# First-phase transfers in program order, planner durations read from the trace, and zeros in shorter gaps

## The chip, the core and the metric

The kernel runs on one core of a Trainium2 chip. The metric is the device time of one execution in microseconds; the time before is the median of three runs, and one further execution was profiled. All matrix work is in 32-bit floats, most of it on TensorE in the rounded form fp32r, where each product is made from three matmuls of split operands.

## The reference, cut to what matters

Two layers of a trunk over 256 latent and 256 context tokens with 1024 features. `c` and `c_ctx` modulate each half of the tokens through nine vectors per layer.

```python
mod_lat = split((silu(c) @ w_mod[l] + b_mod[l]), 9)          # likewise mod_ctx from c_ctx
def macaron_half(x, mods, gain, w_in, w_out):
    shift, scale, gate = mods
    h = modulate(rms_norm(x, gain), shift, scale)
    gate_, up = split(h @ w_in, 2)                            # FFN_DIM = 2816
    return x + 0.5 * gate * ((silu(gate_) * up) @ w_out)
for l in range(2):
    x   = macaron_half(x,   mod_lat[0:3], ...)                # first FFN, both streams
    ctx = macaron_half(ctx, mod_ctx[0:3], ...)
    y_lat, y_ctx = hybrid_mixer(...)                          # 8 attention heads + 4 gated delta-rule heads
    x = x + mod_lat[5] * (y_lat @ w_out[l])
    x = macaron_half(x, mod_lat[6:9], ...)                    # second FFN (context too in layer 0)
```

So before the first FFN matmul the kernel needs the norm statistics of `x`, and the first two modulation vectors (shift and scale), which take 8 MB of `w_mod`.

## The kernel before, in words

**A recorder and a planner.** The program text doesn't issue instructions. `Recorder` notes each instruction as a node with its engine, its duration by `cost_of` and its dependencies; `Schedule.run` then plays all engines forward in modelled time (durations from `cost_of`, the time from one engine's end to another's start from `LAT`, TensorE's two speeds from `Clock`) and picks, whenever an engine is free, the ready node with the lowest priority number. For TensorE this is its rank; for the other engines it is a due time worked back from the matmuls that need the result (`due_times`). `plan` does this 7 times with 3 window sizes and keeps the plan that ends first in the model. `emit` then issues all nodes sorted by their planned start. On the chip each engine runs its own list in that order and waits on semaphores, so the planned times themselves are gone: only the order on each engine, and the buffer that each tile got, remain. All DMAs are issued from the one list of SyncE (SP); a modelled DMA keeps "sync" busy for its bytes at the modelled rate, and its readers may start `LAT["sync"]` later.

**Zeros.** Where the plan leaves TensorE idle for longer than `WARM[1]` us, `keep_warm` puts matmuls of a zero tile (256 columns, counted at 0.109 us each) over a share `WARM[2]` of the gap, to hold the clock up.

**The first phase** is laid out by `main` and the start of `program`. `x` comes in 8 transfers of 256 KB; `square_sum`, `norm_stats` and `norm_spread` make the norm factors `bs`. `features(q, d, n)` handles n blocks of 128 features: `mods_first` loads its share of the first two modulation vectors' weights (4 or 8 transfers of 256 KB into `n` tiles), multiplies them with `sc` (the silu of `c`, from the small `cc` transfer), copies the result out on ScalarE, transposes it, adds the bias from `sm` (the transfer `small`) and scales the gain into `na` on VectorE; `norm_apply` then makes the FFN's operand `h` of these features, split into `hh` and `hl` (tag `s`). There are five such calls: two of one block, three of two. In between, `load(part, units)` brings quarters (256 KB) of the first FFN's input weights for units 0, 1 and 2, which ScalarE (`wh`) and VectorE (`wl`) split. The first group of `ffn` then multiplies feature block by feature block: 48 products of three matmuls each, 6 for each of the 8 blocks, of which blocks 2p and 2p+1 need the quarter `part` = p.

**The order of the first phase's DMAs before** is the planner's: by due time, not by the order in the text.

**The other stretches.** After the first phase come the first FFN, the mixer (attention and delta rule, with many small steps on ScalarE and VectorE between the matmuls), the second FFN, and the same for layer 1. While the FFNs run, `mods` fills in the other modulation vectors: 512 KB of `w_mod` for each of 128 pieces into a `wr` buffer (4 buffers, shared with all weights), reduced on VectorE into `md` by `tensor_tensor_reduce` (the rows show it as CUSTOM_DVE_ANT_0 with output `junk`). At the end of an FFN `add_x`, `square_sum` and `norm` make the next operand.

**Constants.** `con` holds ten constant matrices; the last, `mbd`, is read by nothing.

Lines of the rows: all recorded instructions are issued from one line (680), zeros from line 672. Tiles are named by their tag, so `ps<-n,sc` is the modulation matmul of the first phase, `ps<-s,wh` and `ps<-s,wl` the FFN's.

Of the kernel before, what the change touches and what calls it, by code (L numbers as in the profile page):

```python
# [87 lines left out]
def consts():  # L88
    i = np.arange(128)
    m, j = i[:, None], i[None, :]  # L90
    b, c = m // 32, j // 32
    mats = [
        m == j, m >= 0 * j,
        m > j, m < j, m <= j, m >= j,
        b == c, (b != c) & (b // 2 == c // 2), b // 2 != c // 2,
        b % 2 == c % 2,
    ]
    return np.concatenate([a.astype(np.float32) for a in mats], axis=1)

# [129 lines left out]
class Recorder:  # L229
# [3 lines left out]

    def __init__(self, cost):
        self.nodes, self.classes, self.open, self.cost = [], {}, None, cost
        self.tag, self.ahead = None, 0
        for e in self.ENGINES:
            setattr(self, e, Engine(self, e))

# [38 lines left out]
    def add(self, eng, ops):  # L278
        n = Node()
        n.i, n.eng, n.ops, n.preds, n.succs, n.syms = len(self.nodes), eng, ops, set(), [], []  # L280
        n.table, n.tag, n.ahead = None, self.tag, self.ahead
        n.cost = sum(self.cost(eng, *o) for o in ops)
        n.port = shares_port(eng, *ops[0])
        n.columns = sum(columns_of(*o) for o in ops) if eng == "tensor" else 0
        writes, reads = [], []
        for name, args, kw in ops:
            views = [a for a in list(args) + list(kw.values()) if isinstance(a, View)]
            outs = [a for a in (args[0], kw.get("accum_out")) if isinstance(a, View)]
            writes += outs
            reads += [v for v in views if all(v is not o for o in outs)]  # L290
            if name == "matmul" and not kw["start"]:
                reads.append(args[0])
            if name == "activation":
                n.table = TABLES.get(args[2].name)
        for v in reads:
            self.read(n, v)
        for v in writes:
            self.write(n, v)
        if eng == "tensor":
            for v in writes:  # L300
                if v.sym.group is not None:
                    n.preds.add(v.sym.group)
                v.sym.group = n.i
        n.preds.discard(n.i)
        for p in n.preds:
            self.nodes[p].succs.append(n.i)
        for v in reads + writes:
            if v.sym not in n.syms:
                n.syms.append(v.sym)
                v.sym.nodes.append(n.i)  # L310
        self.nodes.append(n)
# [58 lines left out]
class Pool:  # L370
# [16 lines left out]
    "vector": {"tensor": 0.2, "vector": 0.13, "scalar": 0.13, "gpsimd": 0.16, "sync": 0.13},  # L387
    "scalar": {"tensor": 0.27, "vector": 0.14, "scalar": 0.14, "gpsimd": 0.17, "sync": 0.14},
    "gpsimd": {"tensor": 0.25, "vector": 0.1, "scalar": 0.1, "gpsimd": 0.1, "sync": 0.1},
    "sync": {"tensor": 2.1, "vector": 2.1, "scalar": 2.1, "gpsimd": 2.1, "sync": 2.1},  # L390
}


WARM = (0.8, 0.6, 0.7)
SLACK = 0.2


# [21 lines left out]
class Schedule:  # L419


    def __init__(self, rec, rank, window, due=None):
        self.rec, self.rank, self.window = rec, rank, window
        self.prio = [r - n.ahead for r, n in zip(rank, rec.nodes)]
        if due:
            self.prio = [d if n.eng != "tensor" else p for p, d, n in zip(self.prio, due, rec.nodes)]
        self.start = [None] * len(rec.nodes)
        self.end = [None] * len(rec.nodes)

# [214 lines left out]
def keep_warm(rec, sched, cls):  # L644
# [6 lines left out]
    pe = sorted((sched.start[n.i], sched.end[n.i]) for n in rec.nodes if n.eng == "tensor")  # L651
    out, last = [], WARM[0]
    for a, b in pe:
# [68 lines left out]
def cost_of(eng, name, a, kw):  # L722

    views = [v for v in list(a) + list(kw.values()) if isinstance(v, View)]
    size = lambda v: int(np.prod(v.shape[1:]))
    if name == "dma_start":
        byts = 512 * max(size(v) * v.shape[0] // 128 for v in views if v.shape)
        return max(0.48, byts / 359e3) if eng == "sync" else 1.04
    if eng == "tensor":
        if name == "transpose":  # L730
            return 0.1095
        n = size(a[2])
        if "float32r" in str(a[2].sym.dtype):
            return 0.12 + max(n - 256, 0) * 0.000437
        if kw.get("tile_position", (0, 0))[1]:
            return 0.02
        return max(2 * n, 256) / 1200 + 0.01
    n = max([size(v) for v in views])
    points = sum(1 for v in views[1:] if size(v) == 1) if n > 1 else 0
    psum = any(v.sym.cls[1] == "ps" for v in views)  # L740
    if eng == "vector":
        if name == "reciprocal":
            return 0.068 + n / 160
        rate = 1920 if name in ("tensor_scalar", "tensor_copy") and not psum else 960
        if name == "memset":
            return 0.01 + n / 960
        return 0.068 + n / rate + 0.06 * min(points, 1)
    if eng == "scalar":
        return (0.05 if psum else 0.093) + n / 1200 + 0.093 * points
    if name == "memset":  # L750
        return 0.03 + n / 1185
    return 0.148 + n / 475
# [41 lines left out]
class Build:  # L794
# [35 lines left out]
    def open(self, ctx):  # L830
        tc, nc = self.tc, self.nc
        F32 = self.F32
        M = self.bass.MemoryType
        rec = self.nc

        def pool(name, bufs, **kw):
            p = ctx.enter_context(tc.tile_pool(name=name, bufs=1, **kw))
            make = lambda shape, nm, dt: p.tile(shape, dt, name=nm, tag=nm, bufs=1)
            return Pool(rec, make, bufs, kw.get("space") == M.DRAM)

        cp = self.cp = pool("cp", 1)
        self.lp = pool("lp", 2)
        self.wp = pool("wp", 1)
        self.sp = pool("sp", 1)
        self.tiny = pool("tiny", 4)
        self.ps = pool("ps", 8, space=M.PSUM)
        self.dram = pool("dram", 2, space=M.DRAM)
        con = self.con = cp.tile([128, 9 * 128 + 64], F32, name="con")
        c = [con[:, 128 * i:128 * i + 128] for i in range(9)]
        self.ident, self.ones, self.gt, self.lt, self.le, self.ge, self.mblk, self.m32, self.m64 = c  # L850
        self.mbd = con[:, 1152:1216]
        self.rope = cp.tile([128, 2, TL], F32, name="rope")
        self.junk = cp.tile([128, D], self.BF16, name="junk")
        self.eps = cp.tile([128, 1], F32, name="eps")
        zero = cp.tile([128, 256], self.BF16, name="zero")
        nc.vector.memset(zero, 0.0)
        nc.idle_work(zero, (id(self.ps), "ps"), F32)
        self.x = [None] * KD

    def load_const(self):  # L860
        nc = self.nc
        nc.sync.dma_start(self.con[:, 256:], self.io["consts"][:, 256:1216])
        nc.sync.dma_start(self.rope, self.io["rope"].rearrange("p (a b) -> p a b", b=TL))
        self.gtlt = self.cp.tile([128, 2, 128], self.F32R, name="gtlt")
        nc.scalar.copy(self.gtlt, self.con[:, 256:512].rearrange("p (a b) -> p a b", a=2))
# [998 lines left out]
    def main(self):  # L1864
        nc = self.nc
        self.acc = {}
        self.cond()
        lc = self.layer_consts(0)
        for d in range(KD):
            self.x[d] = self.slot("x", "x")  # L1870
            nc.sync.dma_start(self.x[d], self.io["xt"][:, d])
        nc.sync.dma_start(self.con[:, :256], self.io["consts"][:, :256])
        for d in range(KD):
            for s in (1, 0):
                self.square_sum(d, s, (nc.vector, nc.gpsimd)[s])
        self.wv.spawn(self.program(lc), 5)
        self.wv.run()

    def program(self, lc):
# [17 lines left out]
        def load(part, *units):  # L1897
            for f in units:
                self.weight_part(u[f][-1], self.io["w1_in"][0, f, part // 2], part % 2)

        def features(q, d, n):
            self.mods_first(lc, q, d, n)
            with self.nc.urgent(100):
                for i in range(2 * q + d, 2 * q + d + n):
                    for s in range(2):
                        self.norm_apply(lc, 0, s, i, bs[s])
        load(0, 0)
        features(0, 0, 1)
        load(0, 1, 2)
        features(0, 1, 1)  # L1910
        load(1, 0, 1, 2)
        features(1, 0, 2)
        for f in range(2):
            u[f].append(self.weight_begin())
        load(2, 0, 1)
        features(2, 0, 2)
        load(3, 0, 1)
        features(3, 0, 2)
        self.load_const()
        yield 0.0, 0.0  # L1920
        for l in range(L):
# [3 lines left out]
            a, b, c = f"a{l}" if l else "a", f"b{l}", f"c{l}"  # L1925
# [37 lines left out]
```

## Time and profile before

| | |
|---|---|
| median of 3 runs | 1949.0 us (1946.32 to 1955.2) |
| the profiled execution, its own time | 1952.2 us |
| its span, first to last instruction | 1950.4 us |
| mean granted TensorE clock | 0.991 |
| TensorE matmul busy | 1901.5 us (97%), 11145 matmuls |
| VectorE busy | 1366.0 us (70%) |
| ScalarE busy | 833.3 us (43%) |
| moved by DMA | 281 MB, 144 GB/s over the span |

Busy time of TensorE includes the zeros. Share of busy time is to be read by stage: in the first 40 us DMA is near its full rate, in the FFNs TensorE never stops, in the mixers VectorE and ScalarE are nearly full at times.

### The profile page before, as it was taken

The numbers are of one execution on the slowest core, as the hardware profiler recorded it, in microseconds if no ns is written. First come the engines' busy times: TensorE is split into PE (matmuls) and PEld (weight loads), VectorE is DVE, ScalarE is ACT, GpSimd is POOL, SyncE is SP. The second block draws the span as 40 slices with busy tenths as digits, with TensorE's granted clock in tenths as the row PEclk, the third lists the DMA queues.
The fourth block names the chain that finished last, engine by engine and source line by source line (L and its number), as shares of the span: only waits on it lengthen the run. The fifth ranks groups of instructions, "written<-read, shape, count | busy, mean of one in ns | idle before, by whom it ended". The sixth has DMA issues, their size and how long they took to land.

```text
span 1950.4 us, 29083 instructions
## 1 busy us (share of the span) xinstructions
PE 1901.5 (97%) x11145; PEld 1617.4 (83%) x11145; DVE 1366.0 (70%) x2776; ACT 833.3 (43%) x1612; POOL 26.9 (1%) x31
## 2 busy tenths in 40 slices
PE   8999999999999999999999999999999989899999
PEld 5888887787886879888888898888889877689999
DVE  5666677799987978666653586556337988986555
ACT  5322221258838455222222342221125974755433
POOL 1000000000001000000000000000000000000000
PEclk9999999999998999999999999999999999999999
DMA  9555555553324213555553245656334243136654
GB/s 329 179 153 160 162 177 175 170 169 117 112 81 117 98 44 95 165 162 179 166 162 102 72 146 179 201 177 203 110 98 147 88 114 109 44 114 201 184 182 122
DMA packets 104474, 280.96 MB, mean 144 GB/s; under 512 B 27024, under 2 KB 30480, under 8 KB 104336
## 3 DMA queue, kind: packets, MB, share of 16 engines
q1 hardware_dynamic: 104336, 279.12, 45.9%
q8 instruction: 87, 1.43, 0.3%
q14 instruction: 51, 0.42, 0.1%
HBM read 270.69 MB, written 8.39 MB: 143 GB/s over the span
## 4 chain that ended last, share of the span: by engine, by line
PE 76%; DVE 13%; ACT 4%; DMA 4%; issue 2%; SPq 0%; DVEq 0%; ACTq 0%
PE ps L680 76%; DVE d L680 3%; DVE n L680 2%; DMA wr<-w_mod 2%; DVE wl L680 2%; ACT d L680 1%; DVE wh L680 1%; ACT n L680 1%; DVE junk L680 1%; ACT wh L680 1%; DVE t L680 1%; DVE s L680 1%; DVE x L680 1%; ACT s L680 1%; ACT L680 1%
## 5 line engine op out<-in xcount | busy, mean ns | idle before, releaser
L680 PE MATMUL ps<-s,wh 128*128 128x512 f32 (+1 forms) x3344 | 912.9, 361 | 1.0 <-DVE s L680 0.5
L680 PEld LDWEIGHTS ps<-s,wh 128*128 128x128 f32 x3344 | 592.8, 189 | 100.3 <-issue 1.4
L680 PE MATMUL ps<-s,wl 128*128 128x512 f32 (+1 forms) x1672 | 603.5, 361 | 0.9 <-DVE wl L680 0.9
L680 ACT CAST wh<-wr 128x1024 fp32r<-128x1024 f32 (+2 forms) x341 | 350.4, 1037 | 479.1 <-PE ps L680 328.6
L680 DVE TENSOR_TENSOR wl<-wr,wh 128x1024 fp32r<-128x1024 f32 (+2 forms) x341 | 408.3, 1208 | 97.1 <-ACT wh L680 93.6
L680 DVE CUSTOM_DVE_ANT_0 junk<-wr,m,sm 128x1024 bf16<-128x1024 f32 x224 | 287.6, 1284 | 235.0 <-DMA wr<-w_mod 231.9
L680 PEld LDWEIGHTS ps<-s,wl 128*128 128x128 f32 x1672 | 314.8, 188 | 48.6 <-DVE wl L680 1.6
L680 PE MATMUL ps<-d,wh 128*128 128x256 f32 (+1 forms) x1344 | 300.4, 319 | 6.9 <-DVE x L680 3.9
L680 PEld LDWEIGHTS ps<-d,wh 128*128 128x128 f32 x1344 | 223.1, 191 | 30.3 <-issue 9.3
L680 PE MATMUL ps<-d,wl 128*128 128x256 f32 (+1 forms) x672 | 212.8, 317 | 1.2 <-DVE wl L680 1.2
L680 PE MATMUL ps<-n,wh 128*128 128x512 f32 (+1 forms) x640 | 178.3, 365 | 0.0
L680 DVE SCALAR_TENSOR_TENSOR x<-ps,hg,x 128x256 f32<-128x256 f32 x224 | 97.4, 478 | 93.2 <-PE ps L680 93.1
L680 ACT ACTIVATE d<-ps 128x512 f32<-128x512 f32 (+2 forms) x108 | 56.9, 529 | 237.1 <-PE ps L680 236.7
L680 PE MATMUL ps<-wh,s 128*128 128x512 f32 (+1 forms) x544 | 154.2, 360 | 0.3 <-DVE s L680 0.3
L680 PEld LDWEIGHTS ps<-d,wl 128*128 128x128 f32 x672 | 128.3, 191 | 9.5 <-DVE wl L680 1.7
L680 PEld LDWEIGHTS ps<-n,wh 128*128 128x128 f32 x640 | 115.4, 189 | 20.8
L680 PE MATMUL ps<-n,wl 128*128 128x512 f32 (+2 forms) x416 | 130.6, 347 | 0.7 <-DVE n L680 0.7
L680 DVE TENSOR_TENSOR d<-d,d 128x256 f32<-128x256 f32 (+29 forms) x310 | 111.6, 381 | 16.6 <-ACT d L680 12.0
L680 PEld LDWEIGHTS ps<-wh,s 128*128 128x128 f32 x544 | 96.4, 188 | 19.5 <-issue 5.2
L680 PE MATMUL ps<-wl,s 128*128 128x512 f32 (+1 forms) x272 | 96.6, 355 | 0.6 <-DVE wl L680 0.6
L680 DVE TENSOR_TENSOR d<-d,ps 128x512 f32<-128x512 f32 (+1 forms) x88 | 54.4, 618 | 58.4 <-PE ps L680 40.6
L680 PEld LDWEIGHTS ps<-n,wl 128*128 128x128 f32 x416 | 71.9, 189 | 10.7 <-issue 0.8
(163 smaller groups left out, 1563.7 us busy)
## 6 DMA issues: line engine op xcount, KB each, us to landing
wr<-w_in SPq DMA_DIRECT2D x171, 512.0 KB, 4.3
wr<-w_mod SPq DMA_DIRECT2D x128, 512.0 KB, 4.0
wr<-w_out SPq DMA_DIRECT2D x104, 512.0 KB, 4.2
wr<-wd SPq DMA_DIRECT2D x24, 512.0 KB, 3.8
n<-w_mod SPq DMA_DIRECT2D x32, 256.0 KB, 5.5
wr<-wg SPq DMA_DIRECT2D x8, 528.0 KB, 3.6
xd<-x SPq DMA_DIRECT2D x16, 256.0 KB, 4.5
x<-xd SPq DMA_DIRECT2D x16, 256.0 KB, 3.6
```

Of the source, the lines that this page charges most:

```text
L680: getattr(eng, name)(*[rv(x) for x in a], **{q: rv(x) for q, x in k.items()})
```

## The change

- `nc.settled` marks the SyncE nodes from the start of `main` to the last `load`: their priority is their place in the text (minus 1e6), ahead of all other DMAs. So these transfers are issued in program order.
- That order is written anew: the first block's modulation weights come first, then the quarters of all three units, then the second block's, and so on; `cc` and `small` come ahead of `x`.
- `LAT["sync"]` goes from 2.1 to 2.8 us (2.1 for DMA after DMA), the modelled DMA rate from 359 to 330 GB/s.
- `cost_of` is changed for the reduction `tensor_tensor_reduce` (from 0.13 to 0.19 us ahead of the elements), for VectorE copies and scalings on fewer than 128 partitions or at most 32 elements (half rate), and for ScalarE on 32 partitions (0.1 us more).
- Gaps longer than 0.3 us (before: 0.6) are filled with zeros, over 85% (before: 70%) of their length.
- `mbd` is dropped: `con` and its transfer are 64 columns narrower (32 KB of 480 KB).

```diff
@@ Recorder
+        self.tag, self.ahead, self.settled = None, 0, False
+        n.settled = self.settled and eng == "sync"
@@ LAT, WARM
-    "sync": {"tensor": 2.1, "vector": 2.1, "scalar": 2.1, "gpsimd": 2.1, "sync": 2.1},
+    "sync": {"tensor": 2.8, "vector": 2.8, "scalar": 2.8, "gpsimd": 2.8, "sync": 2.1},
-WARM = (0.8, 0.6, 0.7)
+WARM = (0.8, 0.3, 0.85)
@@ Schedule
+        self.prio = [n.i - 1e6 if n.settled else p for p, n in zip(self.prio, rec.nodes)]
@@ cost_of
-        return max(0.48, byts / 359e3) if eng == "sync" else 1.04
+        return max(0.48, byts / 330e3) if eng == "sync" else 1.04
-        rate = 1920 if name in ("tensor_scalar", "tensor_copy") and not psum else 960
+        parts = min(v.shape[0] for v in views)
+        if name == "tensor_tensor_reduce":
+            return 0.19 + n / 960
+        rate = 1920 if name in ("tensor_scalar", "tensor_copy") and not psum and parts == 128 and n > 32 else 960
-        return (0.05 if psum else 0.093) + n / 1200 + 0.093 * points
+        return (0.05 if psum else 0.093) + n / 1200 + 0.093 * points + (0.1 if views[0].shape[0] == 32 else 0.0)
@@ Build.open, load_const
-        con = self.con = cp.tile([128, 9 * 128 + 64], F32, name="con")
+        con = self.con = cp.tile([128, 9 * 128], F32, name="con")
-        self.mbd = con[:, 1152:1216]
-        nc.sync.dma_start(self.con[:, 256:], self.io["consts"][:, 256:1216])
+        nc.sync.dma_start(self.con[:, 256:], self.io["consts"][:, 256:1152])
@@ main, program
+        nc.settled = True
         self.cond()
...
-        load(0, 0)
         features(0, 0, 1)
-        load(0, 1, 2)
+        load(0, 0, 1, 2)
         features(0, 1, 1)
+        features(1, 0, 2)
         load(1, 0, 1, 2)
-        features(1, 0, 2)
+        features(2, 0, 2)
         for f in range(2):
             u[f].append(self.weight_begin())
         load(2, 0, 1)
-        features(2, 0, 2)
+        features(3, 0, 2)
         load(3, 0, 1)
-        features(3, 0, 2)
+        self.nc.settled = False
         self.load_const()
```

## Rows read from the trace of the kernel before

**Rows 1.** Busy time by stretch: length, PE, PEld, DVE, ACT, POOL, clock, DMA share, GB/s
```profile
0.00:12.41 12.41, 9.56 (x67) 7.49 (x67) 5.31 (x10) 9.26 (x20) 5.54 (x11) 1.00 0.85 285
12.41:39.85 27.44, 22.80 (x365) 14.28 (x366) 15.54 (x49) 12.01 (x30) 0.00 (x0) 0.88 1.01 349
39.85:300.00 260.15, 260.15 (x1124) 212.03 (x1123) 171.78 (x248) 74.92 (x96) 0.00 (x0) 1.00 0.55 172
300.00:412.00 112.00, 102.86 (x509) 87.02 (x508) 90.42 (x154) 30.34 (x44) 1.31 (x4) 0.97 0.52 165
412.00:700.00 288.00, 275.43 (x1749) 229.44 (x1748) 257.83 (x731) 196.63 (x504) 12.54 (x8) 0.98 0.37 110
700.00:1500.00 800.00, 800.00 (x4113) 677.41 (x4110) 486.73 (x780) 252.39 (x370) 1.30 (x4) 1.00 0.45 141
1500.00:1765.00 265.00, 248.76 (x1706) 207.98 (x1705) 233.44 (x671) 182.82 (x450) 6.24 (x4) 0.99 0.34 102
```

**Rows 2.** DMA issues on SP's list in the first phase, in order of time
```profile
18.18 0.43 SPq L680 DMA_DIRECT2D sm<-small  x1
...
19.74 0.33 SPq L680 DMA_DIRECT2D wr<-w_in  x1
...
26.87 0.33 SPq L680 DMA_DIRECT2D wr<-w_in  x1
27.57 3.65 SPq L680 DMA_DIRECT2D n<-w_mod  x6
31.50 3.90 SPq L680 DMA_DIRECT2D wr<-w_in  x6
```

**Rows 3.** VectorE in order of time: its wait for the transfer small
```profile
22.73 0.24 DVE L680 TENSOR_TENSOR md<-d,sm 128x4 f32<-128x4 f32 x2 [2.59 <-DMA sm<-small]
```

**Rows 4.** Groups of TensorE instructions between 12.41 and 39.85 us
```profile
L680 PE MATMUL ps<-n,sc 128*32 128x128 f32 (+1 forms) x320 | 12.3, 296 | 2.6 <-DMA n<-w_mod 2.6
L680 PE MATMUL ps<-s,wh 128*128 128x512 f32 x14 | 5.6, 481 | 0.0
...
L672 PE MATMUL ps<-zero 128*128 128x256 bf16 x12 | 2.1, 318 | 0.0
```

**Rows 5.** TensorE in order of time, first phase
```profile
16.54 3.70 PE L680 MATMUL ps<-n,sc 128*32 128x64 f32 x120
...
39.85 0.62 PE L680 MATMUL ps<-s,wh 128*128 128x512 f32 x2
...
40.55 0.62 PE L680 MATMUL ps<-s,wh 128*128 128x512 f32 x2
```

**Rows 6.** Chain of waits: the last of the eight transfers of x
```profile
4.01 6.07 DMA x<-xt
```

**Rows 7.** Groups of VectorE instructions between 12.41 and 50 us
```profile
L680 DVE SCALAR_TENSOR_TENSOR s<-d,md,s 128x256 fp32r<-128x256 f32 x16 | 7.3, 480 | 1.0 <-ACT s L680 1.0
L680 DVE SCALAR_TENSOR_TENSOR d<-x,na,d 128x256 f32<-128x256 f32 x16 | 7.0, 477 | 0.1
L680 DVE TENSOR_TENSOR wl<-wr,wh 128x512 fp32r<-128x512 f32 x10 | 6.6, 687 | 1.5 <-ACT wh L680 1.5
```

**Rows 8.** TensorE's waits, 290 to 410 us: total, times, longest
```profile
PE ps L680 <- DVE d L680: 4.0, 1, 4.0
PE ps L680 <- DVE x L680: 3.9, 1, 3.9
```

**Rows 9.** VectorE in order of time, ahead of TensorE's stall near 385 us
```profile
380.94 1.28 DVE L680 CUSTOM_DVE_ANT_0 junk<-wr,m,sm 128x1024 bf16<-128x1024 f32 x1 [3.96 <-DMA wr<-w_mod]
```

**Rows 10.** DMA issues: KB each, median us from issue to landing
```profile
wr<-w_mod SPq DMA_DIRECT2D x128, 512.0 KB, 4.0
```

**Rows 11.** Busy time by stretch, the worst 25 us of the second mixer
```profile
1550.00:1575.00 25.00, 19.40 (x101) 15.92 (x102) 24.91 (x102) 23.94 (x77) 0.00 (x0) 0.88 0.26 82
```

**Rows 12.** Zeros on TensorE by stretch: length, busy (count), clock, DMA share, GB/s
```profile
412.00:700.00 288.00, 2.97 (x24) 0.98 0.37 110
...
1500.00:1765.00 265.00, 5.98 (x47) 0.99 0.34 102
```

**Rows 13.** TensorE in order of time: a burst of zeros and what came after it
```profile
428.76 1.81 PE L672 MATMUL ps<-zero 128*128 128x256 bf16 x15
...
431.14 0.51 PE L680 MATMUL ps<-wh,s 128*128 128x264 f32 x2 [0.33 <-DVE s L680]
```

More of the change, by code (lines that the diff above doesn't have):

```diff
@@ L95, in consts @@
         b == c, (b != c) & (b // 2 == c // 2), b // 2 != c // 2,
-        b % 2 == c % 2,
     ]
@@ L235, in __init__ @@
         self.nodes, self.classes, self.open, self.cost = [], {}, None, cost
-        self.tag, self.ahead = None, 0
+        self.tag, self.ahead, self.settled = None, 0, False
         for e in self.ENGINES:
```

## The prediction

> **What bounds the kernel now.** I read the busy time by stretch first, cut where TensorE changes its manner [rows 1]. The reader is to see two kinds of stretch. From 39.85 to 300 us and from 700 to 1500 us TensorE never stops, at a clock of 1.00, the upper of its two levels of 1.2 and 2.4 GHz: 1060 of 1950 us are matmuls back to back, and no order of the same matmuls makes them shorter. All that an order can give back lies in the other stretches. Their idle time is length minus busy: 2.9 us to 12.41, 4.6 to 39.85, 9.1 from 300 to 412, 12.6 from 412 to 700, 16.2 from 1500 to 1765. To that comes what the lower clock costs, length times one minus the clock: 3.3 us (12.41 to 39.85), 3.4 (300 to 412), 5.8 (412 to 700), 2.7 (1500 to 1765). So about 45 us idle and 15 us of clock, some 60 us or 3%, is the most that the change could work on, and much of it is waiting that no order removes.
>
> Next I read the first phase in order of time, on SP's list and on TensorE. DMA is full: 349 GB/s at a share of 1.01 from 12.41 to 39.85 [rows 1]. The planner let the modulation weights run ahead: of the ten quarters of FFN weights only two went out before the last `w_mod`, at 19.74 and 26.87, and `small` only at 18.18 [rows 2], so that VectorE stood 2.59 us for it and made the first block's scale at 22.73 [rows 3]. TensorE did 14 `ps<-s,wh` matmuls, so 7 of the FFN's 48 products, before 39.85 [rows 4], and from there one product each 0.70 us (40.55 minus 39.85) [rows 5].
>
> **The change part by part.** *The order of the first phase.* First the bytes, with 0.262 MB for 256 KB. Moved by 12.41 us: 12.41 x 285 = 3.54 MB; then 0.349 MB per us [rows 1]. In the new order 2.33 MB (`cc`, `small`, `x`, the first part of `con`) are followed by 4 `w_mod` (3.38 MB), 3 quarters (4.16), 4 `w_mod` (5.21), 8 (7.31), 3 quarters (8.09), 8 `w_mod` (10.2), 2 quarters (10.7), 8 `w_mod` (12.8), 2 quarters (13.3). These are moved at 12, 14.2, 17.2, 23, 25.4, 31.5, 33, 39 and 40.5 us. A transfer counts as landed later: the last of `x` was there at 10.08 [rows 6], though its 2.1 MB at 285 GB/s are moved by 7.4, so I add 2.5 us. Before, the last `w_mod` had 2.33 + 8.39 + 2 x 0.262 = 11.2 MB with it and ahead of it, moved at 34.5, so the last features come 4.5 us later than now (41.5 against 37). That is the price. From landing to operand I count 1.5 us (matmuls, copy, transpose, bias, gain) and, for each block, four VectorE steps of 0.48 us less their overlap, 1.7 us [rows 7]. So the blocks are ready at about 18, 22.5, 29, 31, 37.5, 39, 45 and 47 us, each with 6 products of 0.70 us, and their quarters landed in time.
>
> What it can give: from 12.41 to 39.85 TensorE was idle for 4.6 us, did zeros for 2.1 us, and its 320 modulation matmuls were busy for 12.3 us, where 320 at the pace of the 120 back to back (3.70 us) take 9.9 [rows 1, 4, 5]. That is 6.7 to 9.1 us of time without product. The new order could fill it, as from 18 us on there is a block to work on. It won't fill all: up to 18 us only the statistics and the first modulations run, which leaves some 2 us empty; products started there may still run at the lower clock (0.88 over the stretch); and VectorE has 7.3 + 7.0 + 6.6 us of these steps [rows 7] and some 3 us of small ones between 17 and 47 us, with single steps that a block waits behind. I take a gain of **4 us**, with 0 and 9.1 as its ends: nothing, if the later last blocks cost what the earlier first ones bring, and all. It goes straight through: TensorE has no idle from 39.85 to 300 us, and what comes in the FFN (units of weights) is loaded at half of DMA's share.
>
> Here a rule of the skill bears on the new modelled rate. The row shows 349 GB/s with DMA full [rows 1], so the old 359 was 3% high and the new 330 is 5% low. The Trainium skill, "DMA: Bandwidth & Descriptors", section Specifications, gives about 358 GB/s as the limit of one core on HBM, which is the old value. By it, an estimate, the 9.8 MB after 12.41 us would be moved 0.7 us sooner than by the row, and the gain would be 4.7 instead of 4 us.
>
> *The modelled latency and durations.* The plan counted a 512 KB transfer as 1.46 + 2.1 = 3.56 us, now 1.59 + 2.8 = 4.39; the trace has 4.0 from issue to landing [rows 10]. So the plan errs to the other side, by as much. What the old error costs is to be seen at 381 us: VectorE stands 3.96 us behind a reduction whose `w_mod` hasn't landed [rows 9], with the split `wl` and the `add_x` steps queued behind it in its list, and TensorE then waits 3.9 us for `x`; soon after it waits 4.0 us for the sum of squares [rows 8]. With later landings planned, VectorE's list has those steps ahead of the reduction. Idle there is 9.1 us in all, which is one bound; the other is 0, since a new plan can set the reductions just as badly. I take **2 us**, half of the first wait.
>
> In the mixers VectorE and ScalarE are nearly full (257.83 and 196.63 of 288 us) [rows 1], and the order of many small steps decides. The durations there become somewhat truer; nothing in the trace says which order comes out. The nearest row for what an order is worth is the worst piece of the second mixer: 5.6 us idle and a clock of 0.88 in 25 us, 3.0 us more [rows 11]. One such stall less or more is 8.6 us, and these are my ends; I take a gain of **1 us**.
>
> *Zeros.* The 71 zeros of the mixers take 9.0 us [rows 12], in seven bursts. A burst of 15 took 1.81 us and was still followed by a wait of 0.33 us [rows 13]: it lay in a real gap, and 85% instead of 70% of it, 18 zeros, would take 2.2 us, about the whole gap. What hides them is the wait for VectorE or ScalarE; without it each burst delays TensorE by its own length. Bounds: 2 us won in clock (of 8.5 lost in both mixers) and, if as many zeros as now are added where no gap is, 9 us lost. I take **0**. `mbd` is 32 KB, 0.1 us of DMA off the path: 0.
>
> **Sum**: 1950.4 - 4 - 2 - 1 = 1943.4 us of span. The profiled execution took 1952.2, 1.8 more than its span, and the median of the runs is 1949.0, 3.2 below it. So 1943.4 + 1.8 - 3.2 = **1942 us**, 0.36% faster. About 0.5%, 9.7 us, is what a measurement of this kernel can tell from no change.
>
> **The rivals.** *The stalls go too.* If the later landings in the plan free VectorE's list, both waits of [rows 8] go (7.9 us), and if the truer durations take away the stall of [rows 11] half (4 us) besides a first phase of 7 us, the sum is 19 us: **1930 us**. For it: these waits follow from landings planned 0.4 us early; against it: the wait for the sum of squares comes from steps that are all in VectorE's list at that time, and no landing.
>
> *Nothing comes of it.* The last blocks come 4.5 us later and TensorE, whose list is in order, holds products of late blocks ahead of work that is ready; the first phase ends as late as now, and the plans of the mixers are no better: **1949 us**. For it speaks that VectorE's 24 us between 17 and 47 us are near to bound; against it that seven of eight blocks would have to wait.
>
> *A new stall in the mixers*, the other side. Their order is drawn anew; a chain step behind a table load or a row of splits on ScalarE stalls TensorE for 3 to 5 us, and the clock falls with it, as now at 1550 us. One costs 8.6 us and cancels the gain. With one in each mixer, and a gain of 4 in the first phase, it is 1949 - 4 + 17 = **1962 us**; from the second on it decides. Against it: of two mixers now, only one has a stall of that size [rows 1, 11].
>
> **How the numbers follow.** Chances: forecast 0.45, stalls gone 0.27, nothing 0.16, new stalls 0.12. The first and last cases set the sign; the forecast's own range, with 1 to 12 us won, is 1937 to 1948, and its lower edge, below 1939.3, adds 0.09 to the faster side. So faster by over 0.5%: 0.36; within: 0.53; slower: 0.11. The range that holds 8 in 10 goes from 1928, past the case of the stalls gone, to 1957, one new stall with nothing won.
>
> **What would show it.** Right: `small` and the quarters ahead of most `w_mod` on SP's list; more than 20 products before 40 us instead of 7, the last `n,sc` matmul at 40 to 43 us, TensorE without gaps from 30 us on, and the first layer's FFN ending 2 to 7 us earlier. Right for the latency: no wait of 3 us or more for `x` near 380 us. Wrong: TensorE waiting after 40 us for late blocks; zeros followed by no wait; a 25 us slice in a mixer at a clock under 0.9 where there was none. The forecast fails most easily in the mixers, where one stall is as large as all that is counted above.

## The result and the profile after

| | before | after |
|---|---|---|
| median of 4 runs each | 1951.2 us (1946.3 to 1955.2) | 1928.9 us (1925.9 to 1930.6) |
| the profiled execution, its own time | 1952.2 us | 1928.0 us |
| its span | 1950.4 us | 1926.0 us |
| mean granted TensorE clock | 0.991 | 0.997 |

The ratio is 0.9885, 95% interval [0.9857, 0.9913]: 1.15% faster, 22 us. The forecast was 1942, its range 1928 to 1957. The time is close to that of the rival "the stalls go too" (1930).

The busy time of the kernel after by stretch, with the columns of [rows 1]. The cuts are the times of before; the kernel after is 11 us ahead of them from 400 us on and 21 to 24 us ahead at the end, so the later lines hold somewhat more work than those of before.

```profile
0.00:12.41 12.41, 11.07 (x82) 8.93 (x82) 4.31 (x10) 8.01 (x20) 4.18 (x10) 1.00 0.81 259
12.41:39.85 27.44, 26.45 (x307) 15.33 (x307) 15.80 (x40) 10.30 (x26) 1.37 (x2) 0.94 1.04 372
39.85:300.00 260.15, 260.15 (x1179) 207.72 (x1179) 182.24 (x269) 75.51 (x98) 0.00 (x0) 1.00 0.57 177
300.00:412.00 112.00, 112.00 (x611) 96.76 (x609) 94.36 (x165) 38.68 (x60) 0.00 (x0) 1.00 0.58 177
412.00:700.00 288.00, 279.64 (x1832) 230.18 (x1831) 261.78 (x748) 195.59 (x517) 13.80 (x12) 0.99 0.33 101
700.00:1500.00 800.00, 799.99 (x4049) 674.94 (x4048) 489.48 (x777) 256.77 (x364) 1.31 (x4) 1.00 0.47 147
1500.00:1765.00 265.00, 252.96 (x1798) 216.12 (x1797) 233.61 (x654) 183.04 (x445) 5.91 (x4) 0.99 0.36 108
```

Four lines differ from [rows 1] where it matters. From 300 to 412 us TensorE was idle for 9.1 us at a clock of 0.97; now it is never idle, at 1.00. From 12.41 to 39.85 us it is busy for 26.45 instead of 22.80 us. In the mixers the idle time falls from 12.6 to 8.4 us (412 to 700) and from 16.2 to 12.0 us (1500 to 1765). The stretches without idle are as they were.

To place the gain in time, four marks of each trace are compared: the first copy of `x` to DRAM (the first FFN of layer 0 is ending), the first RECIPROCAL at the end of the second FFN of layer 0, the last copy of `x` (first FFN of layer 1) and the first store of `out`. Before they stand at 406.2, 1115.8, 1500.5 and 1938.5 us, after at 394.9, 1094.0, 1479.5 and 1914.1. So 11.3 us are won up to the end of the first FFN, 10.5 in the first mixer with the FFN behind it, none (0.8 lost) in the next FFN, 3.4 in the second mixer with the last FFN.

**The first phase.** SP's DMA issues of the kernel after, in order of time, in place of [rows 2]:

```profile
1.18 0.42 SPq L681 DMA_DIRECT2D sm<-small  x1
1.65 3.74 SPq L681 DMA_DIRECT2D x<-xt  x8
...
6.09 2.97 SPq L681 DMA_DIRECT2D n<-w_mod  x4
9.35 1.67 SPq L681 DMA_DIRECT2D wr<-w_in  x3
...
21.00 1.70 SPq L681 DMA_DIRECT2D wr<-w_in  x3
23.10 4.95 SPq L681 DMA_DIRECT2D n<-w_mod  x8
28.34 1.03 SPq L681 DMA_DIRECT2D wr<-w_in  x2
29.72 5.00 SPq L681 DMA_DIRECT2D n<-w_mod  x8
```

The order is the one written out: three quarters go out at 9.35 us, and the last `w_mod` ends its issue at 34.7 us. TensorE of the kernel after, in order of time:

```profile
20.36 0.32 PE L681 MATMUL ps<-n,sc 128*32 128x64 f32 x8 [0.31 <-DMA n<-w_mod]
20.61 0.73 PE L681 MATMUL ps<-s,wh 128*128 128x512 f32 x2
21.17 0.40 PE L681 MATMUL ps<-s,wl 128*128 128x512 f32 x1
...
42.72 0.74 PE L681 MATMUL ps<-s,wh 128*128 128x512 f32 x2
43.30 0.40 PE L681 MATMUL ps<-s,wl 128*128 128x512 f32 x1
43.62 0.43 PE L681 MATMUL ps<-n,sc 128*32 128x128 f32 x8
43.98 0.74 PE L681 MATMUL ps<-s,wh 128*128 128x512 f32 x2
...
51.14 0.43 PE L681 MATMUL ps<-n,sc 128*32 128x128 f32 x8
```

The first product comes at 20.61 us, and from there nothing in the listing is followed by a gap. But products and modulation matmuls alternate one by one, and this lasts to 51 us. A group of eight is one weight block: four matmuls of the program, two records each in the trace. One product with one such block takes 43.98 - 42.72 = 1.26 us, while a product alone takes 0.70 [rows 5]. The FFN's group in the kernel before, then groups of TensorE's instructions of the kernel after, 0 to 60 us:

```profile
L680 PE MATMUL ps<-s,wh 128*128 128x512 f32 x72 | 23.7, 411 | 0.0
```
```profile
L681 PE MATMUL ps<-s,wh 128*128 128x512 f32 x75 | 26.2, 430 | 0.0
...
L681 PE MATMUL ps<-n,sc 128*32 128x128 f32 x192 | 10.2, 284 | 0.0
```

With two such matmuls to a product that is 37.5 products by 60 us after, and 36 before: the idle time was filled, and 1.5 products, 1.05 us, came of it. The three traces that share the first phase of before (before and the runs zeros_only and reduce_later below) have 35 to 36 products by 60 us, the four with the order written out alone or with other parts (first_only, no_lat, null_a2, after) 37.5 to 39. But two plans of before drawn anew, with no edit there (null_before and null_b3), have 38 and 37. So the gain is small even beside what a new plan brings by itself.

**The end of the first FFN.** VectorE in order of time around the place of [rows 9], first in the kernel before, behind its wait of 3.96 us, then in the kernel after:

```profile
382.76 1.22 DVE L680 TENSOR_TENSOR wl<-wr,wh 128x1024 fp32r<-128x1024 f32 x1
383.89 3.22 DVE L680 SCALAR_TENSOR_TENSOR x<-ps,hg,x 128x256 f32<-128x256 f32 x8
```
```profile
376.50 2.15 DVE L681 SCALAR_TENSOR_TENSOR x<-ps,hg,x 128x256 f32<-128x256 f32 x5
378.57 1.27 DVE L681 CUSTOM_DVE_ANT_0 junk<-wr,m,sm 128x1024 bf16<-128x1024 f32 x1
379.77 0.08 DVE L681 DVE_READ_ACCUMULATOR2_ANT md<- 128x1 f32 x1
379.77 1.26 DVE L681 SCALAR_TENSOR_TENSOR x<-ps,hg,x 128x256 f32<-128x256 f32 x3
380.95 1.25 DVE L681 TENSOR_TENSOR wl<-wr,wh 128x1056 fp32r<-128x1056 f32 x1
```

Before, eight adds to `x` had piled up behind the reduction and the split and ran in a row from 383.89 us. After, the adds run in threes and fives between the reductions, none of which waits here. The groups of the reductions, 60 to 400 us, before and after (total and mean time, then VectorE's idle time ahead of them and what ended it):

```profile
L680 DVE CUSTOM_DVE_ANT_0 junk<-wr,m,sm 128x1024 bf16<-128x1024 f32 x96 | 123.2, 1284 | 95.4 <-DMA wr<-w_mod 93.4 <-DVE x L680 0.4
```
```profile
L681 DVE CUSTOM_DVE_ANT_0 junk<-wr,m,sm 128x1024 bf16<-128x1024 f32 x98 | 125.7, 1283 | 34.3 <-DMA wr<-w_mod 32.8
```

VectorE stood 93.4 us for landings of `w_mod` and now stands 32.8. Both of TensorE's waits of [rows 8] are gone; no other took their place before 410 us.

### The profile page after: what moved, and what is told of

Its sections match the earlier page's. It is cut to its first block, busy times and chain, and to the rows that moved or that the text cites. A ratio compares the mean times of both kernels' runs of the same rounds, so it can differ in the third digit from the quotient of the medians.

```text
span 1926.0 us, 29126 instructions
## 1 busy us (share of the span) xinstructions
PE 1899.7 (99%) x11168; PEld 1607.2 (83%) x11168; DVE 1369.8 (71%) x2776; ACT 830.6 (43%) x1610; POOL 26.6 (1%) x31
## 4 chain that ended last, share of the span: by engine, by line
PE 86%; DVE 6%; ACT 6%; DMA 1%; issue 1%; SPq 0%; DVEq 0%; ACTq 0%
PE ps L681 86%; ACT n L681 2%; DVE n L681 2%; ACT d L681 1%; DVE wh L681 1%; ACT wh L681 1%; DVE s L681 1%; ACT s L681 1%; DMA n<-w_mod 1%; DVE wl L681 1%; ACT L681 1%; DVE d L681 0%; DVE mx L681 0%; DVE t L681 0%; DVE wr L681 0%
## 5 line engine op out<-in xcount | busy, mean ns | idle before, releaser
L681 DVE TENSOR_TENSOR d<-d,d 128x256 f32<-128x256 f32 (+28 forms) x310 | 111.5, 381 | 14.2 <-ACT d L681 9.5
```

Source lines behind the costliest of these rows:

```text
L681: getattr(eng, name)(*[rv(x) for x in a], **{q: rv(x) for q, x in k.items()})
```

## The experiments

Every kernel computes the whole reference. Those made from the kernel after (all but reduce_later, reduce_ready, null_before and null_b3) lack `mbd` as well. Each was timed against the kernel before on the same chip (1951.1, 1952.2 and 1951.0 us in the three sets), and the ratios are to it. Where a plan is drawn anew, any edit moves many instructions. Each expectation spells out its theories; the leading one was that VectorE's list waited for landings because the plan had them too early.

**first_only.** The kernel before with the program order and the new interleaving of the first phase alone.

```diff
+        self.prio = [n.i - 1e6 if n.settled else p for p, n in zip(self.prio, rec.nodes)]
```

> The kernel before with only the order of the first phase changed (transfers in program order, interleaved anew); the planner's durations and the zeros stay as they were. Theory 1, the stalls come from landings planned too early: a gain of 1 to 4 us, VectorE still waits some 200 us in total for w_mod, and TensorE still stands 3 us or more near 385 us. Theory 2, the early start of the FFN lets its loads run ahead and so removes the later stalls too: a gain of 10 us or more, and TensorE's waits between 290 and 410 us fall from 9.1 us to under 3. Theory 3, any new plan scatters: a change of either sign by 5 to 10 us, out of the mixers.

Measured: 1949.4 us, 0.9986 [0.9975, 0.9996]. There are 38 products by 60 us. Of the stall, waits of 5.3 and 1.2 us are left. The first copy of `x` comes at 402.4 us, 3.8 earlier, of which 9.1 - 6.5 = 2.6 us are idle time between 300 and 412 us; so some 1.2 us are left for the first phase itself. One trace doesn't tell them from nothing: zeros_only has the same order of work as before, and its first copy comes at 407.5, 1.3 us from that of before.

**lat_only.** The kernel before with the modelled landing and rate alone.

```diff
-    "sync": {"tensor": 2.1, "vector": 2.1, "scalar": 2.1, "gpsimd": 2.1, "sync": 2.1},
+    "sync": {"tensor": 2.8, "vector": 2.8, "scalar": 2.8, "gpsimd": 2.8, "sync": 2.1},
-        return max(0.48, byts / 359e3) if eng == "sync" else 1.04
+        return max(0.48, byts / 330e3) if eng == "sync" else 1.04
```

> The kernel before with only the modelled landing (2.8 us and 330 GB/s). Theory 1: 12 to 20 us faster, VectorE's waits for w_mod at about 100 us instead of 232, no stall of TensorE over 2 us between 290 and 410 us, and the first phase as before (7 products by 39.85 us). Theory 2: 5 us or less. Theory 3: either sign, and the fall of VectorE's waits doesn't go with a fall of TensorE's.

Measured: 1929.7 us, 0.9876 [0.9855, 0.9896], as fast as the whole change. Its line of 300 to 412 us:

```profile
300.00:412.00 112.00, 112.00 (x618) 97.02 (x617) 94.40 (x165) 39.45 (x62) 1.32 (x4) 1.00 0.59 181
```

The stall is gone without any edit of the first phase, and 40 products are done by 60 us, more than with the order written out. So the first phase was drawn anew too (11 products by 39.85 us, where the expectation had 7), and part of this gain may lie there.

**zeros_only.** The kernel before with zeros in gaps over 0.3 us, over 85% of them. The order of all other work is that of before.

```diff
-WARM = (0.8, 0.6, 0.7)
+WARM = (0.8, 0.3, 0.85)
```

> The kernel before with only the zeros in shorter gaps (0.3 us, 85%); the order of all other instructions is that of before. Theories 1 and 2: within 3 us of before, since zeros stand in gaps that are there. If the higher clock is worth something by itself, 3 to 8 us faster with a clock of 0.995 instead of 0.991; if the new bursts stand where there is no gap, up to 9 us slower.

Measured: 1953.1 us, 1.0005 [0.9993, 1.0016]. Zeros by stretch, with the columns of [rows 12]:

```profile
412.00:700.00 288.00, 3.62 (x30) 2.77 (x30) 0.00 (x0) 0.97 0.37 110
1500.00:1765.00 265.00, 7.46 (x59) 5.45 (x59) 0.00 (x0) 0.98 0.34 100
```

18 more zeros lie in the mixers, 2.1 us. The clock is no higher for them (0.97 and 0.98, before 0.98 and 0.99), and the time no shorter.

**reduce_later.** The plan of the kernel before, kept; only VectorE's list is changed, each reduction going behind the step planned right after it.

```diff
+        if n.ops[0][0] == "tensor_tensor_reduce":
+            key[n.i] += 1.31
```

> The kernel before with its plan as it was, and only VectorE's list changed: each reduction of w_mod is moved behind the one step that was planned right after it, where one was. No other engine's order changes. Theory 1: VectorE no longer holds up that step for the landing; TensorE's waits between 290 and 410 us (9.1 us) fall by 3 to 8 us, and the time by 3 to 10 us. Theories 2 and 3: no change beyond 2 us, as these steps aren't late for TensorE.

Measured: 1947.1 us, 0.9973 [0.996, 0.9987]. TensorE's wait for `x` is gone, the wait for the sum of squares stays; TensorE's one wait between 290 and 410 us in this kernel:

```profile
PE ps L684 <- DVE d L684: 3.1, 1, 3.1
```

The first copy of `x` comes 6.0 us earlier, as much as TensorE's idle time fell (9.1 to 3.1). So the place of the reductions in VectorE's list is what makes most of the stall: nothing else was changed, and the other engines work through the same order in both traces. The eight adds still run in a row, but from 376.18 us, 7.7 us earlier, and VectorE's waits for `w_mod` from 360 to 410 us fall from 10.3 to 4.3 us.

**reduce_ready.** The kernel before, planned anew with only the readers `tensor_tensor_reduce` of a transfer allowed 0.83 us later; all other durations and landings are old.

```diff
-    ready[j] = max(ready[j], en + LAT[e][m.eng])
+    ready[j] = max(ready[j], en + LAT[e][m.eng] + (0.83 if e == "sync" and m.ops[0][0] == "tensor_tensor_reduce" else 0.0))
```

> The kernel before, planned anew with one difference: the reductions of w_mod (and nothing else that reads a transfer) are counted as ready 0.83 us later. Theory 1a, the reductions planned too early make all of the gain: 18 to 25 us faster, no idle TensorE from 300 to 412 us. Theory 1b, the reductions make the gain in the FFN and the later landings of the small transfers that of the mixers: 8 to 13 us faster, and the time from the first copy of x to DRAM (which opens the mixer of layer 0) to the end as before. Theory 3: any size, with the stalls near 385 us still there.

Measured: 1936.3 us, 0.992 [0.99, 0.9941]. No idle from 300 to 412 us, the first copy of `x` at 393.2 us, 13 earlier; VectorE's wait for `w_mod` falls from 231.9 to 90.9 us over the whole kernel. The gain of the first FFN is there in full, that of the mixers is not. That is the pattern of theory 1b, at a size (0.8%, 16 us) between the two theories.

**no_lat.** The kernel after with the old landing and rate.

```diff
-    "sync": {"tensor": 2.8, "vector": 2.8, "scalar": 2.8, "gpsimd": 2.8, "sync": 2.1},
+    "sync": {"tensor": 2.1, "vector": 2.1, "scalar": 2.1, "gpsimd": 2.1, "sync": 2.1},
```

> The changed kernel with the old modelled landing (2.1 us and 359 GB/s). Theory 1: the gain is lost, within 5 us of before, VectorE waits over 200 us for w_mod in total, and stalls of TensorE of 3 us or more come back between 290 and 410 us. Theory 3 (the other durations can bring the same): 10 us or more faster than before.

Measured: 1929.5 us, 0.9887 [0.9866, 0.9908], as fast as after. Here the theory that the truer landing is needed fell. VectorE's waits for `w_mod` of this kernel (total, times, longest), and its line of 300 to 412 us:

```profile
DVE junk L681 <- DMA wr<-w_mod: 202.7, 98, 5.6
```
```profile
300.00:412.00 112.00, 112.00 (x616) 96.95 (x615) 94.83 (x167) 40.17 (x62) 0.00 (x0) 1.00 0.57 176
```

VectorE waits for landings nearly as long as before (202.7 against 231.9 us), and TensorE has no gap all the same. So the sum of VectorE's waits doesn't set the time. What differs is which steps stand behind a wait: the lines of cost_only below show it, and no_lat has the same steps in the same order there.

**no_first.** The kernel after with the first phase of before: the old order in the text, and its transfers by due time.

```diff
-        nc.settled = True
...
+        load(0, 0)
         features(0, 0, 1)
-        load(0, 0, 1, 2)
+        load(0, 1, 2)
```

> The changed kernel with the first phase as before: planner's order of the transfers, old interleaving. If the first phase brings its 1 to 4 us here too, 1 to 4 us slower than the changed kernel. If the new interleaving costs what it brings (it lets modulation matmuls alternate with products up to 51 us), equal or up to 4 us faster than the changed kernel, with 38 or more products by 60 us instead of 37.

Measured: 1935.3 us, 0.9913 [0.9895, 0.9931], 5 to 6 us slower than after, more than either branch of the expectation. Its groups of TensorE, 0 to 60 us:

```profile
L673 PE MATMUL ps<-zero 128*128 128x256 bf16 x163 | 22.3, 287 | 1.3 <-DVE zero L681 1.3
L681 PE MATMUL ps<-s,wh 128*128 128x512 f32 x63 | 20.4, 403 | 0.0
```

Planned with the new durations, the old order brings 31.5 products by 60 us instead of 36; the gaps are filled with zeros. So the written order is worth 1 us against the plan of before and (37.5 - 31.5) x 0.70 = 4.2 us against the plan that would stand here without it.

**grouped.** The kernel after, with the modulation matmuls of the first phase issued four weight blocks at a time (32 records of the trace) instead of one (8). It tests what the alternation costs.

```diff
             for i in range(e):
-                w = raw[:, i].rearrange("p (d j c) -> p j d c", d=nd, j=4)
-                with nc.bundle():
...
+                held.append((k + i, raw[:, i].rearrange("p (d j c) -> p j d c", d=nd, j=4)))
+            if len(held) == 4:
+                with nc.bundle():
+                    for kk, w in held:
...
+                held = []
```

> The changed kernel with the first phase's modulation matmuls issued in groups of four weight blocks instead of one, so that they alternate with products a quarter as often. If each alternation costs TensorE some 0.3 us (a product with one group between takes 1.26 us, where 0.70 and 0.25 would do), 3 to 7 us faster than the changed kernel and 41 or more products by 60 us. If the pace is set by the landing of the weights instead, no change, 37 to 38 products.

Measured: 1922.5 us (1919.0 to 1924.5), 0.9843 [0.9824, 0.9862], the fastest kernel here, 6.4 us below after by the medians and 8 by the ratios. TensorE in order of time, and its groups of 0 to 60 us:

```profile
31.68 1.08 PE L681 MATMUL ps<-n,sc 128*32 128x128 f32 x32
32.70 0.73 PE L681 MATMUL ps<-s,wh 128*128 128x512 f32 x2
...
34.99 1.08 PE L681 MATMUL ps<-n,sc 128*32 128x128 f32 x32
36.00 0.72 PE L681 MATMUL ps<-s,wh 128*128 128x512 f32 x2
```
```profile
L681 PE MATMUL ps<-s,wh 128*128 128x512 f32 x94 | 30.1, 401 | 0.0
...
L681 PE MATMUL ps<-n,sc 128*32 128x128 f32 x192 | 6.5, 276 | 0.0
```

From 32.70 to 36.00 us, three products and one group of 32 take 3.30 us. Less 3 x 0.70 the group takes 1.20 us, 0.30 for each block of eight, where a block between two products took 1.26 - 0.70 = 0.56. For the 24 blocks of [128 x 128] matmuls that is 24 x 0.26 = 6.2 us, and the first product starts 0.6 us sooner (20.01). There are 47 products by 60 us, 9.5 more than after: 9.5 x 0.70 = 6.7 us, and the first copy of `x` comes 6.9 us earlier (388.0). The gain is all of the first phase.

**cost_only.** The kernel before with the truer durations of `cost_of` alone (the reduction 0.06 us longer, small and narrow steps longer).

```diff
+        if name == "tensor_tensor_reduce":
+            return 0.19 + n / 960
```

> The kernel before with only the truer durations (the reduction counted at 0.19 us and its elements, small and narrow steps longer). After the last runs, in which the gain stayed without the modelled landing: theory 4, these durations remove the stall at the FFN's end as the landing does, because the reduction is the commonest step there and was counted short: 10 us or more faster, TensorE idle for less than 2 us from 300 to 412 us. Theory 1: no more than 5 us, stall still there; then it was the first phase together with the durations that did it in the kernel without the modelled landing.

Measured: 1933.5 us, 0.9906 [0.9891, 0.992]. Its line of 300 to 412 us:

```profile
300.00:412.00 112.00, 112.00 (x608) 96.49 (x607) 93.14 (x162) 38.07 (x58) 0.00 (x0) 1.00 0.56 175
```

The stall is gone with the old landing, while VectorE still waits 195.1 us for `w_mod`. So either correction, of the landing or of the durations, is enough for this place. VectorE in order of time there:

```profile
372.53 1.65 DVE L681 SCALAR_TENSOR_TENSOR x<-ps,hg,x 128x256 f32<-128x256 f32 x4
374.10 1.28 DVE L681 CUSTOM_DVE_ANT_0 junk<-wr,m,sm 128x1024 bf16<-128x1024 f32 x1
```

These four adds open the last run of adds of this FFN. They stand ahead of the reduction, and neither it nor those behind it wait for a landing up to 395 us. In the kernel before, three reductions (at 372.62, 373.95 and 380.94 us) come ahead of the same run, which opens at 383.89, two of them behind a wait for their landing.

**null_before, null_b3, null_a2.** Three plans drawn anew for no reason: one latency of the model is moved by 1.5 to 4% (from ScalarE to TensorE 0.27 to 0.28, from TensorE to ScalarE 0.2 to 0.205, both on the kernel before; from VectorE to VectorE 0.13 to 0.132 on the kernel after). They tell a lucky draw from an effect. The first of them:

```diff
-    "scalar": {"tensor": 0.27, "vector": 0.14, "scalar": 0.14, "gpsimd": 0.17, "sync": 0.14},
+    "scalar": {"tensor": 0.28, "vector": 0.14, "scalar": 0.14, "gpsimd": 0.17, "sync": 0.14},
```

> The kernel before with a change that means nothing: ScalarE's result counted as at TensorE after 0.28 instead of 0.27 us, so that the plan is drawn anew in places. Theory 3, the plan of before was an unlucky draw and most others are better: 10 us or more faster, no stall at the FFN's end. Theories 1 and 4, true durations are needed: within 6 us of before, with 5 us or more idle from 300 to 412 us.

> A second such change to the kernel before: TensorE's result counted as at ScalarE after 0.205 instead of 0.2 us; more of the order differs than in the first one. Theory 3: 10 us or more faster, no stall at the FFN's end. Theories 1 and 4: within 6 us of before, stall there.

> The changed kernel with a change that means nothing: VectorE's result counted as at VectorE after 0.132 instead of 0.13 us. If the changed kernel's time is typical of its durations: within 8 us of it (0.985 to 0.993 of before), no stall at the FFN's end. If it was a lucky draw: slower than 0.993.

Measured: 1952.7 us, 1.001 [0.9999, 1.0021]; 1946.4, 0.9976 [0.9965, 0.9987]; 1927.9, 0.9878 [0.9861, 0.9894]. TensorE's waits from 290 to 410 us in null_before:

```profile
PE ps L680 <- DVE x L680: 5.3, 1, 5.3
```

Both new plans of before have the stall (4.8 us for `x` in null_b3), the new plan of after has none. So the stall isn't an unlucky draw; it belongs to the old numbers. The 5 us of null_b3 come from the second mixer.

The marks of these traces side by side, in us (the first mixer is counted from the first copy of `x` to the RECIPROCAL, the second from the last copy of `x` to the first store of `out`):

| kernel | ratio | first copy of x | first mixer and FFN | second mixer and FFN |
|---|---|---|---|---|
| before | 1 | 406.2 | 709.6 | 438.0 |
| null_before | 1.001 | 406.4 | 706.4 | 440.5 |
| null_b3 | 0.9976 | 406.4 | 709.0 | 432.2 |
| zeros_only | 1.0005 | 407.5 | 707.4 | 439.2 |
| reduce_later | 0.9973 | 400.2 | 709.8 | 439.6 |
| first_only | 0.9986 | 402.4 | 709.2 | 438.2 |
| reduce_ready | 0.992 | 393.2 | 707.3 | 437.6 |
| cost_only | 0.9906 | 396.2 | 706.4 | 431.2 |
| lat_only | 0.9876 | 392.9 | 703.0 | 433.4 |
| no_lat | 0.9887 | 393.8 | 701.6 | 430.5 |
| no_first | 0.9913 | 399.9 | 699.8 | 433.8 |
| null_a2 | 0.9878 | 394.5 | 703.9 | 430.2 |
| after | 0.9885 | 394.9 | 699.1 | 434.6 |
| grouped | 0.9843 | 388.0 | 698.6 | 432.9 |

## Why the prediction was right and where it was not

**What bounds the kernel: right.** All that was won came out of the idle time and the clock counted there; the FFN of layer 1 between the marks changed by 0.8 us. The list of stretches there ends at 1765 us; the last 11.9 us, from the first store of `out` on, hold 3.5 us of idle time in both kernels.

**The first phase: forecast 4 us, measured 1 to 1.5.** Its mechanism was seen (SP's order, the first product at 20.61 us where it was 28.80, no gaps), but its two signs of size failed: 16 products instead of more than 20 by 39.85 us, and the last modulation matmul at 51 instead of 40 to 43 us. The step that failed is the one that counted 320 modulation matmuls at the pace of those back to back, 9.9 us in any order, 0.25 for a block of eight. The new order puts them one block at a time between products, and there a block costs 0.56 us: 0.31 x 24 blocks of [128 x 128] matmuls, 7.4 us. The idle time was filled with this. The run grouped, where a block costs 0.30, gives most of it back. VectorE's chain and the late last blocks, the doubts named there, were no limit.

The sentence on the Trainium skill ("DMA: Bandwidth & Descriptors", Specifications, about 358 GB/s for one core) would have made the gain 4.7 us. The row now is 372 GB/s over 27 us at a share of 1.04, above both that figure and the 349 of before, so neither was a ceiling here; TensorE was the limit.

**Landing and durations, first FFN: forecast 2 us, measured about 10.** The term was mis-sized. Of its bounds 0 and 9.1 us I took half of the first wait. All 9.1 us went, and with them the 3.4 us of lower clock, which the term left out: 12.5 us, of which 10 show at the first mark (11.3 less the 1 to 1.5 of the first phase), which lies ahead of the end of that stretch. The argument that the wait for the sum of squares has no landing ahead of it held for most of that wait: in reduce_later the wait for `x` goes and this one stays, at 3.1 of 4.0 us. What failed is the step from there to a wait that stays. It lies in the order of VectorE's steps, and a plan with a truer landing or truer durations orders these anew too: in all such plans here it is gone, but for 0.3 us in no_first. At which of the steps, stays open. Nor was it a reason for a small gain that the new landing errs to the other side: late as it is planned, lat_only has no stall, and an early one costs only where steps that TensorE needs stand behind it in the list (in no_lat TensorE never waits there).

That cost_only has adds ahead of the reduction is shown; why the planner puts them there is argued only: a reduction counted longer leaves VectorE's modelled time fuller, and the adds are then due ahead of it. Which of the durations does it was not tried alone.

**The mixers: forecast 1 us, measured 10.5 and 3.4.** The term was mis-sized, and its ends of 8.6 us either way were too near: they were the price of one stall, while [rows 1] has 12.6 us idle and 5.8 of clock in the first mixer alone. The worst piece of the second mixer [rows 11] is milder, as the rival had it. The kernel after, 1525 to 1550 and 1550 to 1575 us:

```profile
1525.00:1550.00 25.00, 21.20 (x131) 17.86 (x130) 24.96 (x104) 25.00 (x89) 0.00 (x0) 0.96 0.19 63
1550.00:1575.00 25.00, 23.15 (x111) 18.88 (x110) 22.43 (x39) 20.55 (x39) 0.00 (x0) 0.97 0.40 115
```

But the 3.4 us lie within what meaningless new plans do there (432.2 and 440.5 for the same numbers), so no cause can be given. In the first mixer the three plans with the old numbers (before and two nulls) take 706.4 to 709.6 us, 708.3 in the mean; the five with the new durations and at least one other part of the change (after, null_a2, no_lat, no_first, grouped) 698.6 to 703.9, 700.6 in the mean. The two sets don't overlap, so this gain is more than a draw. The landing alone gives 703.0, the durations alone 706.4 and the reductions' landing alone 707.3, each one plan with a scatter of 3 to 5 us.

What the 10.5 us consist of can be read from TensorE between the two marks, before and after:

```profile
406.20:1115.80 709.60, 697.03 (x3983) 587.08 (x3983) 522.03 (x1162) 333.98 (x713) 12.54 (x8) 0.99 0.40 124
```
```profile
394.90:1094.00 699.10, 690.74 (x3972) 580.00 (x3972) 523.17 (x1165) 330.38 (x711) 13.80 (x12) 1.00 0.41 125
```

Idle time with the zeros in it (3.0 and 1.8 us) falls from 15.6 to 10.2 us. The granted clock was 0.5, the lower level, for 16.0 us of the stretch before and for 3.4 after, which loses half of each, 8.0 and 1.7 us. So more than half of this gain is clock. In one trace each, idle time and zeros are 13.9 to 15.8 us in the eight kernels with the old durations (lat_only and reduce_ready among them), and 10.2 to 12.1 in the six with the new ones (cost_only among them): this part goes with the durations. The clock goes with no single number: it costs 10.2 us in cost_only, 6.8 in reduce_ready, 3.4 in lat_only and in no_lat, and 0 to 5.1 in the four others with the new durations, where the six other kernels with the old ones lose 6.0 to 9.8. At which steps either part is won stays open.

**Zeros and `mbd`: forecast 0.** Right (1.0005): zeros_only has both parts, and `mbd` was not tried by itself.

**The chances.** The rival that came had 0.27, and the range held because its lower edge was drawn for that rival; 1928.9 lies 0.9 us inside it. The forecast itself had 7 us, a third of the 22 measured. The rival's total came out near, not its parts: it had 7 us in the first phase, 7.9 for the two waits and 4 in the mixers, and the marks show about 1, 10 and 13.9. Errors of both signs cancel there, which is luck. The three terms of the forecast were each a cautious middle between bounds; two of them lay on the same planner numbers, so both went to the favourable side together, that of the mixers past its end.

## What to carry to other kernels

When an order comes from a model and each engine runs it as a fixed list, look for the wait on a landing that has a backlog behind it in the same list, and ask what in the backlog the bounding engine needs, since the total of that list's waits says little (no_lat has 202.7 us of them for `w_mod`, the kernel after 96.0, and they take 1929.5 and 1928.9 us). Before crediting a re-planned order with a few microseconds, draw a plan or two with a meaningless change; here that alone moved the time by up to 0.24%. And when small matmuls are spread into the gaps of a full engine, price them by their pitch among the others, not by their pitch in a run.

## What was not expected of the hardware

A block of eight fp32 matmul records with 128 x 32 weight tiles and 128 columns adds 0.56 us where it stands alone between fp32r products of 512 columns (kernel after), and 1.20 us, 0.30 a block, where four blocks stand together (grouped), both at a clock of 1.00. An estimate from these two: some 0.35 us for each change to and fro, and 0.21 for each block. Why the change costs this was not tried. And one core's DMA moved 372 GB/s over 27 us in the kernel after, 349 in the kernel before with the same queues; what made the difference was not tried.
